# The small block of decays and betas in a hybrid decoder layer: three matmuls a k-tile become two

## The chip, the cores and the metric

The kernel runs on one core of a Trainium2 chip. The metric is the time of one execution on the device in microseconds (us). Before the change three runs gave 2778.44, 2771.64 and 2778.57 us, with a median of 2778.44 us.

The core's engines work side by side, each through its own queue in order: TensorE (PE in the profile; its loading of weights is PEld) multiplies matrices into PSUM, VectorE (DVE) and ScalarE (ACT) work element by element, GpSimd (POOL) does a few small things, and SyncE (SP) issues all the DMA transfers.

## What is computed

One layer with parallel mixers over 2048 tokens and a model width of 1024. A combined projection of the normed input feeds four heads of gated DeltaNet and four of HGRN2; their outputs are concatenated and projected, and an MLP and a gated per-layer embedding follow. The part that matters here are the eight columns of the projection that give each of the four DeltaNet heads its decay and its beta:

```
hn = rms_norm(h, pre_mix_norm)
proj = einsum('btd,dc->btc', hn, w_in)
a_gdn = proj[..., OFF_GDN_A:OFF_GDN_B]      # 4 columns, one a head
b_gdn = proj[..., OFF_GDN_B:OFF_HG_F]       # 4 columns, one a head
beta  = sigmoid(b_gdn)
g_dec = -exp(gdn_a_log) * softplus(a_gdn + gdn_dt_bias)
o_a   = gated_delta_rule_chunked(q_a, k_a, v_a, g_dec, beta)   # uses cumsum(g_dec) inside each chunk
```

All is in float32. A matmul that takes its operands in the rounded form float32r is cheaper but less exact, so the kernel splits every operand into a high part (the value rounded to float32r) and a low part (what the rounding left), both float32r, and sums products of parts.

## The kernel before

**Tiles.** Tokens are cut into four quarters of 512 (`QT`), the 1024 input features into eight k-tiles of 128 (`KD`). The normed input of a quarter stands in eight tiles `xt`, each with a high and a low part side by side. A block of the projection is 128 output columns for one quarter: a bank of PSUM (`mm`) of 128 x 512 receives, for each k-tile, three matmuls: high weights by high input, high weights by low input, low weights by high input. That makes 24 matmuls.

**The list of blocks.** `works` holds, for each quarter, first the block "ab" (decays and betas) and then 32 blocks, eight for each pair of a DeltaNet and an HGRN2 head. [...]

**Weights.** In the first quarter a block's weights are loaded raw, split on ScalarE (a rounding copy, line 163) and VectorE (a subtraction, line 164), and the split tile is stored to DRAM for later (`keep`, line 179). In the other three quarters the split tile is loaded back (`reload`, line 184). There are three buffers for split tiles, so a reload waits until the block three earlier has been multiplied and stored.

**The order of the work.** The orders of TensorE and of SP are written by hand; those of VectorE, ScalarE and GpSimd come from a planner that estimates when each instruction is ready. TensorE's order is woven by a clock: each block is cut into three pieces, and after each piece `tick()` runs the steps that an agenda holds for that beat (and `half()` those for the middle of a piece). The steps of the heads' mixers are generators with fixed beats (`A_STEPS`, `B_STEPS`). So the mixers' small matmuls stand at fixed places among the projection's matmuls, and where a step's input is late, TensorE waits with everything behind it. When the block ab of a new quarter is multiplied, the last DeltaNet head of the quarter before is still in its triangular solve (`pr`, `xs`, lines 662 to 672, on VectorE). Its result goes out to DRAM (`xd`, line 677) and comes back rearranged (`xt`, line 684), VectorE transposes it (`xn`, line 686), and TensorE uses it (`psp`, line 691). The heads that have just finished are normed (`finish`: `og`, `osq`, and `norm_steps`: `hl`, `nrm`, lines 263 and 264).

**From the block to the decays.** `decays` (from line 463) runs in the last beat of the block and in three later ones. ScalarE reads rows 0 to 3 of the bank and adds the bias (`sp`, line 468), VectorE clears the tile `gb` of 36 x 512 (line 469), ScalarE reads rows 32 to 35 and writes their tanh into `gb` (line 470). A softplus follows: `se` = max(-sp, sp) on VectorE (472), an exponential and a logarithm on ScalarE (473, 474; each may need a load of its function's table, ACT_TABLE_LOAD), max and add on VectorE (475), a factor (476), and four running sums along the tokens into `gb` (478). Rows 0 to 3 of `gb` go to DRAM (`gd`, line 482); a copy with part of the tokens turned round (`gbb`, 485) and four small transposes on TensorE (`ps_gb`, 488), due four beats after the block, bring all 36 rows to columns (`gcol`).

The first quarter's block runs right after the start-up in which embeddings are computed: its DMA queue still carries stores of these (`ed`), and VectorE clears the mixers' tiles (lines 417 to 426) once they have landed.

Of the kernel before, what the change touches and what calls it, by code (L numbers as in the profile page):

```python
# [10 lines left out]
F32 = mybir.dt.float32  # L11
# [73 lines left out]
def trunk(ctx, tc, x, xT, pT, vecs, w_in, w_ab, gdn_a_log, gdn_dt_bias, w_out, w_up, w_down,  # L85
# [319 lines left out]
    with mixers as mctx:  # L405
# [6 lines left out]
        def mt(name, tag, bufs=1, shape=(P, NC, P)):  # L412
            return mp.tile(list(shape), F32, tag=tag, name=name, bufs=bufs)
# [49 lines left out]
        def decays(ps, q):  # L463

            gb = mt(f"gb_{q}", "gb", 1, (36, QT))
            sp = m2.tile([4, QT], F32, tag="tmp", name=f"sp_{q}")
            se = m2.tile([4, QT], F32, tag="th", name=f"se_{q}")
            S.activation(sp, ps[0:4, :], AF.Identity, bias=dec[:, 1:2])
            V.memset(gb, 0.0)
            S.activation(gb[32:36, :], ps[32:36, :], AF.Tanh, scale=0.5)  # L470
            V.tensor_scalar(gb[32:36, :], gb[32:36, :], 0.5, 0.5, ALU.mult, ALU.add)
            V.scalar_tensor_tensor(se, sp, -1.0, sp, ALU.mult, ALU.max)
            S.activation(se, se, AF.Exp, scale=-1.0)
            S.activation(se, se, AF.Ln, bias=1.0)
            V.scalar_tensor_tensor(sp, sp, 0.0, se, ALU.max, ALU.add)
            V.tensor_scalar(sp, sp, nexpa, None, ALU.mult)
            for c in range(NC):
                V.tensor_tensor_scan(gb[0:4, blk(c)], one[0:4, :], sp[:, blk(c)], 0.0, ALU.mult, ALU.add)
            gd = dr.tile([4, QT], F32, name=f"gd{q}")
            decay[q] = [gd, None]  # L480
            yield
            nc.sync.dma_start(gd, gb[0:4, :])
            yield
            back = mt(f"gbb_{q}", "gbb", 1, (36, QT // 2))
            V.tensor_copy(back.rearrange("p (n b i) -> p n b i", b=NB, i=SB), odd_back(gb))
            ps = bank(f"ps_gb_{q}", ph)
            for c in range(NC):
                PE.transpose(ps[:, c * 36 : (c + 1) * 36], back[:, blk(c // 2)] if c % 2 else gb[:, blk(c)],
                             ident[:36, :36])
# [435 lines left out]
        last = t + LAST  # L925
        staged, split_w = {}, {}

        def stage_work(j):

            if j < len(works) and works[j][3] == 0:  # L930
                staged[j] = stage(works[j][0], works[j][2])

        def split_work(j):

            if j < len(works):
                split_w[j] = staged.pop(j)() if j in staged else reload(works[j][1], works[j][0])

        def keep_work(j):
            if works[j][3] == 0:
                keep(works[j][1], split_w[j])  # L940

        def load_x(q):
# [68 lines left out]
        with tc.manual_schedule(engines={mybir.EngineType.SP}):  # L1011
            stage_work(0)
            stage_work(1)
            split_work(0)
            stage_work(2)
            split_work(1)
            for j, (name, key, src, q, h, then, g, b) in enumerate(works):
                split_work(j + 2)
                stage_work(j + 3)
                keep_work(j)  # L1020
                ps = bank(f"mm_{name}")
                w, xt = split_w.pop(j), xts[q]
                terms = []
                for k, xk in enumerate(xt):
                    terms += [(w[:, 0, k, :], xk[:, 0, :]), (w[:, 0, k, :], xk[:, 1, :]), (w[:, 1, k, :], xk[:, 0, :])]
                nt = len(terms)
                for s in range(SPT):
                    for i in range(s * nt // SPT, (s + 1) * nt // SPT):
                        if i == (2 * s + 1) * nt // (2 * SPT):
                            half()  # L1030
                        PE.matmul(ps, *terms[i], start=i == 0, stop=i == nt - 1)  # L1031
# [12 lines left out]
            at(clock[0], mix_operands(0), (1, 2, 3, 4, 6, 7, 9, 11))  # L1044
            call(clock[0] + 2, partial(stage_out, 0))
            call(clock[0] + 5, partial(ready_out, 0))
            call(clock[0] + 6, partial(stage_out, 1))
            call(clock[0] + 13, partial(ready_out, 1))
            call(clock[0] + 14, partial(stage_out, 2))
            held = {}  # L1050

            def first_outs():

                for j in range(2):
                    ps = held[j] = bank(f"mmo_0_{j}")
                    w = ready.pop(j)
                    for i in range(3 * KD):
                        k, term = i // 3, i % 3
                        PE.matmul(ps, w[:, term // 2, k, :], xin[0][k][:, term % 2, :], start=i == 0, stop=i == 3 * KD - 1)
                        if i % 8 == 7:  # L1060
                            yield

            outs = first_outs()
            while clock[0] <= last or len(held) < 2 or 1 in ready:
                if fill:
                    q, d = fill.pop(0)
                    new = embed_tile(q, d, ple[d // 4], pts[q], accs, m2, 2)
# [12 lines left out]
                tick()  # L1080
            for _ in outs:
                tick()
# [661 lines left out]
```

## Time and profile before

| | |
|---|---|
| median of three runs | 2778.44 us (2771.64 to 2778.57) |
| span of the profiled execution | 2778.2 us (a time of that execution apart from its span is not given) |
| TensorE busy | 2696.7 us, 97% |
| VectorE busy | 2048.2 us, 74% |
| ScalarE busy | 1471.2 us, 53% |
| matmuls on the block ab | 96 in four blocks, from 44.8, 303.9, 574.6 and 832.4 us |
| bytes moved by DMA | 589.24 MB |

Times in the profile are counted in us from the span's start. A row of the timeline gives start, length, engine, line, operation, output and inputs by the program's names, and in brackets the idle time just before the instruction with what ended it. In the chain of waits a row is one link of the chain that ended last. A matmul's own length in a row is its latency; matmuls follow each other faster than that, since they are pipelined. Windows give each engine's busy time in a stretch, and the clock that TensorE was granted as a share of full speed.

### The profile page before, as it was taken

The page shows a single profiled execution, that of the slowest core. Times are in us where ns is not written, and L with a number is a line of the kernel's source. Part 1 is how long each engine was busy: PE and PEld are TensorE (multiplying, and loading weights), DVE is VectorE, ACT ScalarE, POOL GpSimd, SP SyncE. Part 2 cuts the span into 40 slices and gives each one's busy share as a digit, 9 for nine tenths or more (in the row PEclk, how much of TensorE's full clock was granted, in tenths as well). Part 3 has the DMA queues.
Part 4 walks back from the last instruction along what each step waited for, and adds up shares of the span by engine and source line. Part 5 has one row for each costly group of instructions (what it writes and reads, how often), then busy time and mean ns, then how long its engine had stood idle before and what let it go on. Part 6 is the DMA issues. An engine that isn't in the chain of part 4 may idle for free.

```text
span 2778.2 us, 38362 instructions
## 1 busy us (share of the span) xinstructions
PE 2696.7 (97%) x12721; PEld 2219.1 (80%) x12721; DVE 2048.2 (74%) x4242; ACT 1471.2 (53%) x2943; POOL 104.2 (4%) x104
## 2 busy tenths in 40 slices
PE   7999999999999999999899999999999999999999
PEld 5787788878888887777688887887888888887887
DVE  6787877787787777578889867758787765567775
ACT  6665554455545445676555545545454455465431
POOL 0000000000000000000000000001000000001000
PEclk9999999999999999999999999999999999999999
DMA  7776776667666665887466547667454446577663
GB/s 261 261 242 217 230 249 220 218 215 244 231 211 215 213 213 166 267 300 241 141 222 217 181 149 252 222 192 247 155 197 145 147 165 210 190 254 246 213 207 118
DMA packets 268598, 589.24 MB, mean 212 GB/s; under 512 B 55642, under 2 KB 59960, under 8 KB 249200
## 3 DMA queue, kind: packets, MB, share of 16 engines
q1 hardware_dynamic: 268400, 586.79, 63.2%
q8 instruction: 101, 1.65, 0.2%
q14 instruction: 97, 0.79, 0.1%
HBM read 419.75 MB, written 166.92 MB: 211 GB/s over the span
## 4 chain that ended last, share of the span: by engine, by line
PE 62%; DVE 9%; DMA 8%; issue 6%; ACT 3%; SPq 1%; POOL 1%; DVEq 0%; POOLq 0%; ACTq 0%
PE u L1100 22%; PE d L1100 20%; PE mm L1031 9%; PE mmg L1100 6%; DMA ud_g<-u_g 2%; DMA sys_g<-ud_g 1%; DVE pr_g L667 1%; DVE xs_g L670 1%; DVE xs_g L672 1%; PE mmo L1100 1%; DMA mixT<-mixd 1%; DMA rsb_g<-rd_g 1%; DMA b<-h1d 0%; DMA rd_g<-m_g 0%; DVE acc_vg L511 0%
## 5 line engine op out<-in xcount | busy, mean ns | idle before, releaser
L1031 PE MATMUL mm<-xt,w 128*128 128x512 f32 x3072 | 787.0, 403 | 1.9 <-ACT qk_h L767 0.9
L1031 PEld LDWEIGHTS mm<-xt,w 128*128 128x128 f32 x3072 | 558.6, 190 | 109.7 <-ACT qk_h L767 1.3
L1100 PE MATMUL d<-db,da 128*128 128x512 f32 x2688 | 613.0, 390 | 3.9 <-DVE db L217 1.9
L1100 PE MATMUL u<-t,wu 128*128 128x512 f32 x2604 | 608.0, 396 | 3.3 <-ACT wu L163 3.3
L1100 PEld LDWEIGHTS d<-db,da 128*128 128x128 f32 x2688 | 503.9, 188 | 112.3 <-DVE db L217 4.7
L1100 PEld LDWEIGHTS u<-t,wu 128*128 128x128 f32 x2604 | 489.5, 188 | 121.2 <-ACT wu L163 4.1
L217 DVE TENSOR_TENSOR db<-db 128x512 fp32r<-128x512 f32 x224 | 161.2, 720 | 72.6 <-ACT db L216 71.7
L1429 DVE TENSOR_TENSOR u<-u,u 128x512 f32<-128x512 f32 x224 | 150.3, 682 | 72.5 <-PE u L1100 71.3
L216 ACT ACTIVATE db<-db 128x512 fp32r<-128x512 f32 x224 | 140.9, 629 | 82.2 <-DMA db<-hid 80.2
L1100 PE MATMUL mmo<-mixT,w_out 128*128 128x512 f32 x720 | 172.9, 401 | 7.2 <-DVE w_out L164 5.8
L1100 PE MATMUL mmg<-h2T,wg 128*128 128x512 f32 x768 | 178.1, 394 | 0.0
L1470 ACT ACTIVATE u<-u 128x512 f32<-128x512 f32 x128 | 81.0, 633 | 179.5 <-DVE u L1429 179.0
L1100 PEld LDWEIGHTS mmg<-h2T,wg 128*128 128x128 f32 x768 | 144.3, 188 | 33.5
L1100 PEld LDWEIGHTS mmo<-mixT,w_out 128*128 128x128 f32 x720 | 137.3, 191 | 41.8 <-DVE w_out L164 7.1
L164 DVE TENSOR_TENSOR da<-da 128x512 fp32r<-128x512 f32 x128 | 92.7, 724 | 90.2 <-ACT da L163 89.8
L163 ACT ACTIVATE da<-da 128x512 fp32r<-128x512 f32 x128 | 80.5, 629 | 137.6 <-DMA da<-sumd 113.0
L163 ACT ACTIVATE wu<-a 128x512 fp32r<-128x512 f32 x124 | 74.1, 624 | 47.9 <-DMA a<-in_w_up_dram 45.1
L667 DVE TENSOR_TENSOR pr_g<-xs_g,sys_g 128x16 f32<-128x16 f32 (+14 forms) x240 | 93.8, 391 | 5.4
L227 POOL TENSOR_TENSOR acc_y<-acc_y,sq_y 128x512 f32<-128x512 f32 x28 | 38.4, 1371 | 1393.3 <-ACT sq_y L226 1393.3
L164 DVE TENSOR_TENSOR wu<-a,wu 128x512 fp32r<-128x512 f32 x124 | 84.7, 686 | 4.9 <-ACT wu L163 4.8
L1471 ACT ACTIVATE u<-u 128x512 f32<-128x512 f32 x128 | 80.8, 631 | 3.7
L672 DVE SCALAR_TENSOR_TENSOR xs_g<-xs_g,sys_g 128x4 f32<-128x4 f32 x256 | 57.6, 225 | 29.3 <-DMA sys_g<-ud_g 23.9
(374 smaller groups left out, 3817.6 us busy)
## 6 DMA issues: line engine op xcount, KB each, us to landing
w<-cache_in SPq DMA_DIRECT2D x96, 1024.0 KB
db<-hid SPq DMA_DIRECT2D x224, 256.0 KB
cache_in<-w SPq DMA_DIRECT2D x32, 1024.0 KB
hid<-u SPq DMA_DIRECT2D x128, 256.0 KB
da<-sumd SPq DMA_DIRECT2D x128, 256.0 KB
a<-in_w_up_dram SPq DMA_DIRECT2D x124, 256.0 KB
hid<-ht SPq DMA_DIRECT2D x96, 256.0 KB
dr<-in_w_down_dram SPq DMA_DIRECT2D x96, 256.0 KB
```

The lines of the kernel that those rows point to most:

```text
L163: S.activation(t[:, 0], raw, AF.Copy)
L164: eng.tensor_tensor(t[:, 1], raw, t[:, 0], ALU.subtract)
L216: S.activation(t[:, 0], plain(t), AF.Copy)
L217: V.tensor_tensor(t[:, 1], plain(t), t[:, 0], ALU.subtract)
L227: eng.tensor_tensor(acc, acc, sq, ALU.add)
L667: V.tensor_tensor(pr[:, :, :, 0:i], xs[:, None, :, 0:i].broadcast_to([P, 2, GC, i]), sys[:, 0:i, i : i + 2].rearrange("p j two -> p two j" ...
L672: V.scalar_tensor_tensor(xs[:, :, i + 1], xs[:, :, i], sys[:, i, i + 1 : i + 2], xs[:, :, i + 1], ALU.mult, ALU.add)
L1031: PE.matmul(ps, *terms[i], start=i == 0, stop=i == nt - 1)
L1100: PE.matmul(ps, a, b, start=start, stop=stop)
L1429: V.tensor_tensor(c[new], c[old], ps, ALU.add)
L1470: S.activation(c[k], c[k], AF.Relu)
L1471: S.activation(c[k], c[k], AF.Square)
```

## The change

The eight real columns leave most of the weight tile empty, and the change uses it: the low parts of columns 0 to 35 are put at columns 64 to 99 of the same tile. One matmul with this tile multiplies an input by high and low weights at once, and the results stand in rows 0 to 35 and 64 to 99 of the bank. So a k-tile takes two matmuls (by high and by low input) where it took three, a block 16 where it took 24; the product of low weights and low input, left out before, is now in it. The tile has half the bytes: its store and its three reloads move 0.5 MB each where they moved 1 MB. In the first quarter VectorE subtracts 36 columns a k-tile where it subtracted 128.

`decays` has to add the two groups of rows first: ScalarE copies rows 64 to 99 into `gb`, VectorE adds rows 0 to 35 of the bank, and `sp` and the tanh then read `gb`. The clearing of `gb` goes, since the empty columns give zeros.

```diff
         def decays(ps, q):
             gb = mt(f"gb_{q}", "gb", 1, (36, QT))
+            S.activation(gb, ps[64:100, :], AF.Copy)
+            V.tensor_tensor(gb, gb, ps[0:36, :], ALU.add)
             sp = m2.tile([4, QT], F32, tag="tmp", name=f"sp_{q}")
             se = m2.tile([4, QT], F32, tag="th", name=f"se_{q}")
-            S.activation(sp, ps[0:4, :], AF.Identity, bias=dec[:, 1:2])
-            V.memset(gb, 0.0)
-            S.activation(gb[32:36, :], ps[32:36, :], AF.Tanh, scale=0.5)
+            S.activation(sp, gb[0:4, :], AF.Identity, bias=dec[:, 1:2])
+            S.activation(gb[32:36, :], gb[32:36, :], AF.Tanh, scale=0.5)
...
+        def stage_ab():
+            raw = wp.tile([P, KD, P], F32, tag="raw", name="raw_ab", bufs=2)
+            nc.sync.dma_start(raw, w_ab)
+            def ready():
+                w = wp.tile([P, KD, P], F32R, tag="whl", name="w_ab0")
+                S.activation(w, raw, AF.Copy)
+                V.tensor_tensor(w[:, :, 64:100], raw[:, :, 0:36], w[:, :, 0:36], ALU.subtract)
+                return w
+            return ready
+        def reload_ab(q):
+            w = wp.tile([P, KD, P], F32R, tag="whl", name=f"w_ab{q}")
+            nc.sync.dma_start(w.bitcast(F32).rearrange("p k n -> p (k n)"), cached["ab"])
+            return w
+        def keep_ab(w):
+            cached["ab"] = dr.tile([P, KD * P], F32, name="cache_ab")
+            nc.sync.dma_start(cached["ab"], w.bitcast(F32).rearrange("p k n -> p (k n)"))
...
                 for k, xk in enumerate(xt):
-                    terms += [(w[:, 0, k, :], xk[:, 0, :]), (w[:, 0, k, :], xk[:, 1, :]), (w[:, 1, k, :], xk[:, 0, :])]
+                    if h is None:
+                        terms += [(w[:, k, :], xk[:, 0, :]), (w[:, k, :], xk[:, 1, :])]
+                    else:
+                        terms += [(w[:, 0, k, :], xk[:, 0, :]), (w[:, 0, k, :], xk[:, 1, :]),
+                                  (w[:, 1, k, :], xk[:, 0, :])]
```

`stage_work`, `split_work` and `keep_work` call these functions where the block is ab, at the places where they called `stage`, `reload` and `keep`.

More of the change, by code (lines that the diff above doesn't have):

```diff
@@ L926, in trunk @@
         staged, split_w = {}, {}
+        def stage_ab():
[14 more added lines that the diff above has]
+            nc.sync.dma_start(cached["ab"], w.bitcast(F32).rearrange("p k n -> p (k n)"))
         def stage_work(j):
             if j < len(works) and works[j][3] == 0:
-                staged[j] = stage(works[j][0], works[j][2])
+                staged[j] = stage(works[j][0], works[j][2]) if works[j][4] is not None else stage_ab()
         def split_work(j):
             if j < len(works):
-                split_w[j] = staged.pop(j)() if j in staged else reload(works[j][1], works[j][0])
+                if j in staged:
+                    split_w[j] = staged.pop(j)()
+                else:
+                    split_w[j] = reload(works[j][1], works[j][0]) if works[j][4] is not None else reload_ab(works[j][3])
         def keep_work(j):
-            if works[j][3] == 0:
+            if works[j][3] == 0 and works[j][4] is None:
+                keep_ab(split_w[j])
+            elif works[j][3] == 0:
                 keep(works[j][1], split_w[j])
@@ L1024, in trunk @@
                 for k, xk in enumerate(xt):
-                    terms += [(w[:, 0, k, :], xk[:, 0, :]), (w[:, 0, k, :], xk[:, 1, :]), (w[:, 1, k, :], xk[:, 0, :])]
+                    if h is None:
+                        terms += [(w[:, k, :], xk[:, 0, :]), (w[:, k, :], xk[:, 1, :])]
+                    else:
+                        terms += [(w[:, 0, k, :], xk[:, 0, :]), (w[:, 0, k, :], xk[:, 1, :]),
+                                  (w[:, 1, k, :], xk[:, 0, :])]
                 nt = len(terms)
```

## The prediction

> **What bounds the kernel now.** I read the page first, then the one tile the change is about, then the order of time on each engine around its four appearances. On the page, TensorE is busy for nearly the whole span, so a matmul removed looks like time gained:
>
> ```profile
> span 2778.2 us, 38362 instructions
> PE 2696.7 (97%) x12721; PEld 2219.1 (80%) x12721; DVE 2048.2 (74%) x4242; ACT 1471.2 (53%) x2943; POOL 104.2 (4%) x104
> ```
>
> But that share is a mean over the kernel. The change touches four short places, one a quarter of the tokens, and there the question is what ends TensorE's next wait. The tile's own view gives the size of the block, the chain of waits the pace of its matmuls:
>
> ```profile
> L1031 PE MATMUL mm_ab<-xt,w_ab x96: 388/392/502, 44.8 to 839.1; 128*128 128x512 f32 x96
> L164 DVE TENSOR_TENSOR w_ab<-raw_ab,w_ab x1: 1224/1224/1224, 25.1 to 25.1; 128x1024 fp32r<-128x1024 f32 x1
> 376.70 5.51 PE mm L1031 x24
> ```
>
> The 392 ns is a matmul's latency; 24 in a row take 5.51 us, so one costs 0.230 us of TensorE. Now the last block (fourth quarter), TensorE first (its last row is the same wait in the third quarter), then VectorE, then ScalarE, each in order of time (start, length, engine, line; the idle time before an instruction and who ended it in brackets):
>
> ```profile
> 837.46 2.08 PE L1031 MATMUL mm_ab<-xt,w_ab 128*128 128x512 f32 x8
> 843.54 0.50 PE L264 MATMUL nrm_g<-hl_g,ones 128*128 128x512 f32 x1
> 849.59 0.71 PE L691 MATMUL psp_g<-xn_g,um 128*128 128x128 f32 x4 [0.54 <-DVE xn_g L686]
> ...
> 591.91 0.71 PE L691 MATMUL psp_g<-xn_g,um 128*128 128x128 f32 x4 [0.56 <-DVE xn_g L686]
> ```
> ```profile
> 811.94 0.23 DVE L672 SCALAR_TENSOR_TENSOR xs_g<-xs_g,sys_g 128x4 f32<-128x4 f32 x1 [0.41 <-DMA sys_g<-ud_g]
> 840.17 0.69 DVE L554 TENSOR_TENSOR og_g<-pso_g,zt_zg 128x512 f32<-128x512 f32 x1
> 840.90 0.70 DVE L556 TENSOR_TENSOR osq_g<-osq_g,q_g 128x512 f32<-128x512 f32 x1
> 841.64 0.67 DVE L472 SCALAR_TENSOR_TENSOR se<-sp 4x512 f32<-4x512 f32 x1
> 842.79 0.69 DVE L164 TENSOR_TENSOR hl_g<-osq_g,hl_g 128x512 fp32r<-128x512 f32 x1
> 846.18 0.68 DVE L475 SCALAR_TENSOR_TENSOR sp<-sp,se 4x512 f32<-4x512 f32 x1 [2.54 <-ACT se L474]
> 849.13 0.41 DVE L686 STREAM_TRANSPOSE xn_g<-xt_g 128x256 f32<-128x256 f32 x1
> ```
> ```profile
> 839.58 0.68 ACT L468 ACTIVATE sp<-mm_ab,dec 4x512 f32<-4x512 f32 x1 [0.37 <-PE mm_ab L1031]
> 840.28 0.59 ACT L470 ACTIVATE gb<-mm_ab 4x512 f32<-4x512 f32 x1
> 841.63 0.63 ACT L163 ACTIVATE hl_g<-osq_g 128x512 fp32r<-128x512 f32 x1 [0.75 <-DVE osq_g L556]
> 845.51 0.63 ACT L474 ACTIVATE se<-se 4x512 f32<-4x512 f32 x1
> ```
>
> This is the heart of the case. The block ends at about 839.4. TensorE's next wait (849.59) is for xn_g, which VectorE makes at 849.13, late because VectorE stood still for 2.54 us until ScalarE had the logarithm (845.51 to 846.14): the block's own chain sp, se, table load, exp, table load, ln, sp, scans, all in order on two engines. And sp's partner se started only at 841.64, although sp was there at 840.26: between 811.94 and 846.18 VectorE's rows show no idle time at all. So VectorE's queue, started by a DMA at 811.94, sets when the chain runs; TensorE arrives early and waits. The third quarter repeats this (its wait for xn_g, at 591.91, is 0.56).
>
> **The change part by part.** *Matmuls.* Four blocks of 24 become 16: 32 x 0.230 = 7.4 us of TensorE, 1.84 us a block. If TensorE bounded everywhere, the sum would be -7.4.
>
> *Copy and add ahead of the chain.* The chain gets two instructions. ScalarE's copy of 36x512 out of PSUM is like the gb row above (0.59). VectorE's add with one operand in PSUM is like og_g (0.69): the bounds are 0.49 (the memset of the same 36x512, below) and 0.70 (osq_g), and I take 0.69, the row nearest in operands. Then sp, no longer from PSUM, as before. What is queued behind: the add waits for ScalarE's copy, that for the block's last matmul; behind the add stand og_g, osq_g or se, behind these hl_g, which the norm matmul (843.54) needs. The block's PSUM bank is let go after the add, no later than before. The memset that they replace ran early, off this stretch:
>
> ```profile
> L469 DVE MEMSET gb<- x4: 485/485/485, 53.0 to 597.0; 36x512 f32 x4
> ```
>
> *Blocks three and four (quarters 2, 3 from 0).* The block ends 1.84 us earlier, the copy falls into ScalarE's idle time, but VectorE is full until se: the add pushes osq_g, hl_g, se and through them both table loads by 0.69. TensorE gains 1.84, waits 1.84 + 0.69 more at hl_g and xn_g: +0.7 each. Bounds: had the planner placed add and se ahead of og_g and osq_g (1.3 us of VectorE), the logarithm comes about 1.3 earlier: -1.3; were VectorE no limit at all, -1.84. If the add lands behind osq_g, sp on ScalarE comes behind hl_g and pays its 0.68 as well: +1.4.
>
> *Block two.* Here two things end VectorE's standing almost together:
>
> ```profile
> 318.46 0.17 DVE L664 COPY xs_g<-cst 128x8 f32<-128x8 f32 x1 [3.22 <-DMA xd_g<-xs_g]
> 317.94 0.63 ACT L474 ACTIVATE se<-se 4x512 f32<-4x512 f32 x1
> 322.71 0.71 PE L691 MATMUL psp_g<-xn_g,um 128*128 128x128 f32 x4 [2.35 <-DVE xn_g L686]
> 304.33 8.67 DMA cache_in<-w
> 313.81 0.32 SPq L677 DMA_DIRECT2D xd_g<-xs_g  x1
> ```
>
> The store xd_g lands at 318.46 because SP's queue stood behind a weight reload whose buffer a store (8.67 us from 304.33) still held. Part by part: the reload of the block's weights before it moves 0.5 MB instead of 1 MB, so this goes earlier and stops mattering; the logarithm's end (317.94 + 0.63 = 318.57) moves to 319.26 with the add, where VectorE was free at some 318.7, after the xs_g copy: +0.5. Bounds -1.84 and +1.2 (the add behind osq_g again).
>
> *Block one.* TensorE waits openly for this chain (TensorE, ScalarE, two rows of VectorE, SP, and a window whose last figure is GB/s):
>
> ```profile
> 62.72 0.32 PE L488 MATMUL ps_gb<-cst,gbb 36*128 36x36 f32 x1 [2.83 <-DVE gbb L485]
> 50.65 0.68 ACT L468 ACTIVATE sp<-mm_ab,dec 4x512 f32<-4x512 f32 x1 [3.48 <-PE mm_ab L1031]
> 50.05 0.09 DVE L417 MEMSET bound<- 128x36 f32 x1 [1.43 <-DMA ed<-e]
> 53.36 0.62 DVE L472 SCALAR_TENSOR_TENSOR se<-sp 4x512 f32<-4x512 f32 x1
> 42.36 0.43 SPq L179 DMA_DIRECT2D cache_ab<-w_ab  x1
> 40.00:46.00 6.00, 5.61 (x23) 3.93 (x22) 4.01 (x7) 5.19 (x10) 0.00 (x0) 1.00 0.87 311
> ```
>
> se waits for memsets (50.05 to 53.3, gb's 0.49 among them), and these for the last ed store, queued behind the 1 MB store of this block's weights at 42.36. Half of that at 311 GB/s is 1.7 us, so the memsets can start when VectorE falls idle, 50.05 - 1.43 = 48.6, and last 2.8 without gb's, to 51.4. Then add to 52.1, sp to 52.8, se at 52.85 against 53.36: -0.5. Bounds: -1.84 (add ahead of the memsets), +0.9 (the store lands as before: 52.85, 53.55, 54.25).
>
> *Costing nothing.* The low half of the first weights becomes 288 columns for 1024, saving under 1 us of the 1.22 at 25.1, but VectorE idles next until the norm's row arrives. If VectorE were not idle there, the saving could count in full. The stores and reloads of half the size keep their places in SP's queue, and TensorE's rows on mm_ab show no wait for a reload; where the queue is the limit, blocks one and two have it above.
>
> **Sum**, against this execution's span of 2778.2 (the median of the runs, 2778.44, is 0.2 above it; no separate time of the profiled execution is given): -0.5 + 0.5 + 0.7 + 0.7 = +1.4, so 2779.6 and, on the runs' median, 2779.8: I say 2780. The 7.4 us of matmuls turn into longer waits at hl_g, xn_g and gbb.
>
> **The rivals.** *One: the clock falls in blocks three and four (the slow side of my forecast).* In the windows the second column is TensorE's busy time, and the row ends with granted clock, DMA share and GB/s:
>
> ```profile
> 59.00:63.00 4.00, 0.53 (x4) 0.41 (x4) 3.67 (x10) 3.06 (x5) 2.33 (x1) 0.73 0.30 42
> 63.00:66.00 3.00, 3.00 (x10) 2.35 (x10) 0.82 (x3) 0.34 (x2) 0.27 (x1) 0.50 1.00 375
> 323.00:326.00 3.00, 3.00 (x16) 2.44 (x16) 3.00 (x8) 2.16 (x7) 0.00 (x0) 0.61 1.01 401
> 326.00:329.00 3.00, 3.00 (x13) 2.42 (x12) 1.88 (x7) 1.43 (x3) 0.00 (x0) 0.82 0.98 287
> 849.00:853.00 4.00, 3.41 (x20) 2.75 (x20) 4.00 (x11) 2.44 (x9) 0.00 (x0) 1.00 0.55 35
> ```
>
> After the waits of block one and two TensorE ran at 0.50 and at 0.61 to 0.82; after the short one of block four at 1.00. Block two's fall cost 3 x 0.39 + 3 x 0.18 = 1.7 us. With 2.5 us more waiting, blocks three and four may fall too: 2779.8 + 3.4 = 2783. Against it: the new wait is split by norm matmuls and 16 projections. [...] Chance 0.18.
>
> *Two: the chain does not hold TensorE (the fast side).* The planner lays out VectorE anew and puts add and se ahead of the group's closing work in every block; what decides is whether se starts up to 1.84 us before 841.64, and likewise in the other blocks. Then each block gives up to 1.84: 2778.4 - 7.4 = 2771. For it: copy and block end come early. Against: VectorE's 32 us without a gap up to the logarithm, and sp now needs two hops more. Chance 0.20.
>
> *Three: the order of ScalarE and VectorE is dealt anew beyond the blocks.* Only TensorE's and SP's orders are written by hand. Two quarters with the same work differ, and of the first one's waits one stands out (total us, times, longest):
>
> ```profile
> 304.00:575.00 271.00, 259.99 (x1400) 220.49 (x1399) 203.22 (x589) 138.18 (x364) 15.38 (x17) 0.98 0.69 230
> 575.00:832.00 257.00, 254.12 (x1393) 216.68 (x1392) 198.91 (x582) 137.46 (x363) 15.04 (x17) 1.00 0.67 226
> ```
> ```profile
> PE psc_g L743 <- ACT w_g L740: 6.9, 4, 4.1
> ```
>
> TensorE idles 11.0 us in the second quarter and 2.9 in the third, and most of the 11.0 is the state recurrence: a matmul (psc_g) waits for ScalarE to scale w_g, behind whatever the planner put ahead of it there. If the third quarter came to look like the second, 8 us come on top: 2788; if the fourth did too, 2796. It decides from about 8 us of such waits more, two of the longest (4.1). Chance 0.12; the same luck the other way, the second quarter like the third, 2780 - 8 = 2772 and with some gain of the blocks 2768, 0.05.
>
> **How the numbers follow.** Forecast 0.45, rivals 0.18, 0.20, 0.12 and 0.05. The forecast alone spans 2777 (blocks a little better) to 2784 (near all upper bounds, 0.9 + 1.2 + 1.4 + 1.4 = +4.9). The range for 8 in 10 runs from 2770.5, the full gain, to 2787.5, the clock's fall on top of the upper bounds. A measurement tells about 0.3%, 8.3 us, from nothing: under 2770.1 lie the lucky layout and part of rival two, 0.12; over 2786.8 the unlucky one and the tails of rival one, 0.20; the rest, 0.68, is no measurable change.
>
> **What would show it.** In the changed profile: 64 matmuls on mm_ab; the block's last matmul some 1.8 us nearer its start; an add on VectorE before sp; the psp_g wait near 849.6 and 591.9 grown (or one at nrm_g) to 2 to 3 us together; the wait for gbb in block one at 4 us or more; granted clock after each block. I am wrong if the waits at psp_g and nrm_g stay at half a microsecond (then the gain stands), if se starts before og_g, or if the third and fourth quarter's lengths move by more than 3 us.

## The result, and the profile after

The changed kernel takes 2784.15 us (median of 16 runs, 2778.66 to 2791.21) and the kernel before, beside it, 2778.79 us (16 runs, 2771.64 to 2787.11): a ratio of 1.002 with an interval of 1.001 to 1.0029, or 2.8 to 8.1 us more. The time lies in the predicted range and within the 0.3% called no measurable change, but 5.4 us above the kernel before where the sum said 1.4. It is rival one's 2783 rather than the forecast's 2780.

The profiled execution of the changed kernel took 2780.20 us, with a span of 2778.3, so 1.9 us lie around the span. Profiled executions of one kernel differ by almost as much as the change is worth: a second one of the kernel before had a span of 2774.1, 4.1 less, and one of the changed kernel 2776.2. So the profiles say where time moved, and the medians how much is left of it. The page and the tile's own view, as before:

```profile
span 2778.3 us, 38301 instructions
PE 2690.7 (97%) x12689; PEld 2215.5 (80%) x12689; DVE 2050.2 (74%) x4242; ACT 1473.2 (53%) x2947; POOL 104.0 (4%) x104
```
```profile
L1063 PE MATMUL mm_ab<-xt,w_ab x64: 388/394/499, 45.1 to 834.6; 128*128 128x512 f32 x64
```

The 32 matmuls are gone, and TensorE's busy time is 6.0 us less. The span is the same. The timeline of TensorE, in the last block (from 829.40) and in the third quarter's (from 567.46), shows what stands there instead:

```profile
839.21 0.50 PE L264 MATMUL nrm_g<-hl_g,ones 128*128 128x512 f32 x1 [0.35 <-DVE hl_g L164]
846.83 0.71 PE L692 MATMUL psp_g<-xn_g,um 128*128 128x128 f32 x4 [2.13 <-DVE xn_g L687]
850.32 0.32 PE L489 MATMUL ps_gb<-cst,gbb 36*128 36x36 f32 x1 [2.15 <-DVE gbb L486]
850.79 6.40 PE L1063 MATMUL mm<-xt,w 128*128 128x512 f32 x16
...
585.13 0.71 PE L692 MATMUL psp_g<-xn_g,um 128*128 128x128 f32 x4 [2.10 <-DVE xn_g L687]
588.62 0.32 PE L489 MATMUL ps_gb<-cst,gbb 36*128 36x36 f32 x1 [2.15 <-DVE gbb L486]
589.08 5.87 PE L1063 MATMUL mm<-xt,w 128*128 128x512 f32 x16
```

The predicted wait is the psp_g row: 0.5 before, 2.1 now. The next wait, at ps_gb, did not exist in these two blocks. And the 16 projections behind it take 6.40 and 5.87 us, where the kernel before took 3.95 in the last block: the clock fell. The kernel before, in the last block:

```profile
851.07 0.23 PE L488 MATMUL ps_gb<-cst,gbb 36*128 36x36 f32 x1
851.35 3.95 PE L1031 MATMUL mm<-xt,w 128*128 128x512 f32 x16
```

The windows around the fall in the changed kernel's last block (TensorE's busy time in the second column; granted clock, DMA share and GB/s at the end):

```profile
846.00:849.00 3.00, 1.34 (x9) 1.10 (x9) 3.00 (x10) 0.86 (x4) 0.00 (x0) 1.00 0.11 38
849.00:852.00 3.00, 1.68 (x6) 1.42 (x7) 2.08 (x8) 2.25 (x4) 0.00 (x0) 0.55 0.59 45
852.00:856.00 4.00, 4.00 (x11) 3.11 (x10) 0.69 (x2) 0.07 (x1) 0.00 (x0) 0.50 0.93 365
```

VectorE and then ScalarE in the last block of the changed kernel show how the chain came to be late:

```profile
836.83 0.67 DVE L557 TENSOR_TENSOR osq_g<-osq_g,q_g 128x512 f32<-128x512 f32 x1
837.75 0.66 DVE L467 TENSOR_TENSOR gb<-gb,mm_ab 36x512 f32<-36x512 f32 x1
839.41 0.67 DVE L473 SCALAR_TENSOR_TENSOR se<-sp 4x512 f32<-4x512 f32 x1
844.67 0.68 DVE L476 SCALAR_TENSOR_TENSOR sp<-sp,se 4x512 f32<-4x512 f32 x1 [1.52 <-ACT se L475]
846.35 0.42 DVE L687 STREAM_TRANSPOSE xn_g<-xt_g 128x256 f32<-128x256 f32 x1
846.71 1.32 DVE L479 TENSOR_TENSOR_SCAN gb<-one,sp 4x128 f32<-4x128 f32 x4
847.96 0.71 DVE L512 SCALAR_TENSOR_TENSOR acc_kg<-mm,cols,acc_kg 128x510 f32<-128x510 f32 x1
...
849.99 0.27 DVE L486 COPY gbb<-gb 36x256 f32<-36x256 f32 x1
```
```profile
837.53 0.63 ACT L163 ACTIVATE hl_g<-osq_g 128x512 fp32r<-128x512 f32 x1 [1.36 <-DVE osq_g L557]
838.45 0.72 ACT L470 ACTIVATE sp<-gb,dec 4x512 f32<-4x512 f32 x1 [0.28 <-DVE gb L467]
839.85 0.59 ACT L266 ACTIVATE osq_g<-nrm_g 1x512 f32<-1x512 f32 x1
840.45 1.28 ACT L474 ACT_TABLE_LOAD   x1
842.28 0.41 ACT L828 ACTIVATE keys_h<-qk_h 128x256 f32<-128x256 f32 x1
844.01 0.63 ACT L475 ACTIVATE se<-se 4x512 f32<-4x512 f32 x1
```

The add stands behind osq_g, and sp behind hl_g. Operations that were not in the chain's way before now are. On ScalarE the pass osq_g (line 266) runs ahead of the exponential's table load (before, it ran at 846.17, behind the logarithm), and keys_h between the exponential and the logarithm's table load. On VectorE two pieces of the convolution (acc_kg) and more stand between the scans and gbb, from 847.96 to 849.99. Counted from each block's first matmul, the last block reads:

| us after the block's first matmul | before | after | difference |
|---|---|---|---|
| last matmul of the block starts | 6.73 | 5.16 | -1.57 |
| logarithm ends | 13.72 | 15.24 | +1.52 |
| psp_g starts | 17.16 | 17.43 | +0.27 |
| scans end | 16.77 | 18.63 | +1.86 |
| gbb starts | 17.87 | 20.59 | +2.72 |
| last ps_gb starts | 18.77 | 21.16 | +2.39 |
| first key product (kk_g) starts | 35.49 | 40.38 | +4.89 |

The block gets 1.6 us shorter, not 1.84 (1.8 in block one, 1.2 in block two). The logarithm is 1.5 later, yet psp_g only 0.3: the planner put the transposition xn_g ahead of the scans (846.35, 846.71), and gbb paid for it. From ps_gb to kk_g another 2.5 us are lost to the clock.

### The profile page after: what moved, and what is told of

It is laid out like the page before. It is cut to its first block, busy times and chain, and to the rows that moved or that the text cites. A ratio compares the mean times of both kernels' runs of the same rounds, so it can differ in the third digit from the quotient of the medians.

```text
span 2778.3 us, 38301 instructions
## 1 busy us (share of the span) xinstructions
PE 2690.7 (97%) x12689; PEld 2215.5 (80%) x12689; DVE 2050.2 (74%) x4242; ACT 1473.2 (53%) x2947; POOL 104.0 (4%) x104
## 4 chain that ended last, share of the span: by engine, by line
PE 63%; DVE 11%; DMA 7%; ACT 4%; issue 4%; SPq 1%; POOL 1%; DVEq 0%; ACTq 0%; POOLq 0%
PE u L1132 22%; PE d L1132 18%; PE mm L1063 11%; PE mmg L1132 6%; DMA ud_g<-u_g 1%; DVE pr_g L668 1%; DMA sys_g<-ud_g 1%; PE mmo L1132 1%; DVE xs_g L671 1%; DVE xs_g L673 1%; DMA rd_g<-m_g 1%; DMA da<-sumd 1%; DVE raw_xt L980 1%; DMA xs<-in_x_dram 1%; DVE xt L164 1%
## 5 line engine op out<-in xcount | busy, mean ns | idle before, releaser
L1132 PEld LDWEIGHTS mmg<-h2T,wg 128*128 128x128 f32 x768 | 144.2, 188 | 33.8 <-issue 0.4
L164 DVE TENSOR_TENSOR da<-dr,da 128x512 fp32r<-128x512 f32 x96 | 66.3, 690 | 18.3 <-ACT da L163 16.3
```

The source lines that it names most:

```text
L164: eng.tensor_tensor(t[:, 1], raw, t[:, 0], ALU.subtract)
L1132: PE.matmul(ps, a, b, start=start, stop=stop)
```

## The experiments

The measure used below is the time from a block's first matmul on mm_ab to the first head's key product kk_g behind it, in the four blocks in turn. A second profile of the kernel before told how far it varies on its own.

| | blocks one to four, us | from block one's kk_g to block two | ratio to before |
|---|---|---|---|
| before | 33.9, 38.3, 35.6, 35.5 | 225.3 | |
| before, second profile | 34.6, 38.1, 35.6, 35.3 | 222.4 | |
| after | 33.4, 39.8, 40.1, 40.4 | 220.1 | 1.0020 |
| after, second profile | 34.1, 40.1, 40.6, 39.7 | 220.3 | |

> The kernel before once more, for a second profile of it. In its first profile the stretches between the blocks (first quarter, second quarter) took 225.3 and 232.4 us, in the changed kernel and the three experiments 217.6 to 220.1 and 226.7 to 229.1. If that difference belongs to the kernel, it is there again; if it was that execution's own (falls of the clock at other places, DMA), this one has about 219 and 228. The times from a block's start to the first head's key products should be the same again: 38.3, 35.6 and 35.5 us in blocks two to four.

The blocks repeat within 0.7 us; the rest of the first quarter does so only within 3. The two stretches between blocks took 222.4 and 230.1 us, between what the two readings said, so how much of their difference belongs to the kernel is left open. The second profile of the changed kernel asked whether its falls of the clock were chance:

> The changed kernel once more, unaltered, for a second profile. Theory A (the granted clock falls in blocks three and four because TensorE has little to do for some 4 us there: the gap ahead of the preparation's transposes, the transposes, the gap ahead of the weights' transposes): the falls behind 586 and 849 us come again within 10 us of those places, and the times from the block's first matmul to the first head's key products are again about 39.8, 40.1 and 40.4 us for blocks two to four (each within 0.7). Theory B (the falls of that one execution were chance): no fall behind one or both of the places, and that block takes about 37 us, as blocks three and four took 38.2 and 36.5 in the kernel with the early copy of the weights' rows.

They came again, at 585.9 and 845.3 us and 6.8 us long each, and the block times with them (block two's fall was 6.8 us for 3.4). Theory A held. The falls are not the profiled executions' own either: over all 16 runs of the changed kernel the mean granted clock is 0.9902, and over the kernel before 0.9928 to 0.9932 beside the experiments.

**The two halves of the change, each alone.** The chain (run e1): copy and add in the kernel before, with its 24 matmuls.

```diff
+            S.activation(gb, ps[64:100, :], AF.Copy)
+            V.tensor_tensor(gb, gb, ps[0:36, :], ALU.add)
-            S.activation(sp, ps[0:4, :], AF.Identity, bias=dec[:, 1:2])
-            V.memset(gb, 0.0)
-            S.activation(gb[32:36, :], ps[32:36, :], AF.Tanh, scale=0.5)
+            S.activation(sp, gb[0:4, :], AF.Identity, bias=dec[:, 1:2])
+            S.activation(gb[32:36, :], gb[32:36, :], AF.Tanh, scale=0.5)
```

> Only the copy and the add are put ahead of the chain; weights, 24 matmuls a block and transfers stay as before (the rows 64 to 99 that are added are zeros here). Theory A (the longer chain makes TensorE wait, and the waits let its clock fall): in blocks two to four the transposes on gb come about 21 us after the block's start, as in the changed kernel, for 18.8 before, whatever the number of matmuls; so 3 x 2.4 us more, block one some 1 us more, and 0 to 2 falls of the clock of 3.4 us each: 2787 to 2795 beside 2779 for the kernel before. Theory B (the two instructions cost what they last, 1.3 us each block, and the matmuls' saving stands in full elsewhere): 2784. Theory C (the two instructions are hidden in a block of 24 matmuls): 2779.

2792.19 against 2777.41 us, a ratio of 1.0056 (1.0038 to 1.0074): +14.8 us, for instructions that last 0.60 + 0.67 us and come four times. Theory A's 2787 to 2795 holds. The blocks took 36.7, 42.1, 41.6 and 41.4. TensorE in the last block, and the window behind:

```profile
849.79 0.71 PE L692 MATMUL psp_g<-xn_g,um 128*128 128x128 f32 x4 [0.81 <-DVE xn_g L687]
855.49 0.32 PE L489 MATMUL ps_gb<-cst,gbb 36*128 36x36 f32 x1 [3.65 <-DVE gbb L486]
```
```profile
856.00:860.00 4.00, 4.00 (x12) 3.17 (x12) 1.85 (x5) 1.22 (x4) 0.00 (x0) 0.57 1.02 426
```

So the loss is the chain's. In this block it sits at gbb (ps_gb is done 4.2 us later than before) and in the clock (1.7 more from there to kk_g), not at psp_g. The matmuls (run e2): two a k-tile, the old chain and the tile of 1 MB.

```diff
-                    terms += [(w[:, 0, k, :], xk[:, 0, :]), (w[:, 0, k, :], xk[:, 1, :]), (w[:, 1, k, :], xk[:, 0, :])]
+                    terms += [(w[:, 0, k, :], xk[:, 0, :]), (w[:, 0, k, :], xk[:, 1, :])]
+                    if h is not None:
+                        terms += [(w[:, 1, k, :], xk[:, 0, :])]
```

> Only the matmuls: 16 a block (the product with the low weights is left out for decays and betas), the chain and the transfers as before. Theory A: in blocks two to four VectorE and the chain still end where they ended, TensorE comes 1.84 us early and waits for it at xn_g and gbb; little is gained, and the wait at psp_g (2.35, 0.56, 0.54 before) grows to 2 to 4 us; with one or two more falls of the clock 2777 to 2784. Theory B: the saving stands, 2771.5 to 2773, and the waits at psp_g stay at half a microsecond in blocks three and four.

2773.51 us, 0.9985 (0.9973 to 0.9996): 3.9 us less. That misses theory A's 2777 to 2784 and is next to theory B's 2773, but the blocks are as theory A had them: 34.2, 39.5, 35.0, 35.0, in sum 143.8 where the kernel before had 143.2 and 143.5. In blocks three and four 0.2 to 0.6 of the 1.84 arrived, in the first two nothing. The gain lies behind blocks one and two (220.0 us for 225.3 and 222.4, 228.1 for 232.4 and 230.1), and no term explains it. One row of TensorE says why the blocks gained so little:

```profile
842.43 0.71 PE L691 MATMUL psp_g<-xn_g,um 128*128 128x128 f32 x4 [1.49 <-DVE xn_g L686]
```

psp_g starts 17.03 us after the block's first matmul, before 17.16: the block's last matmul comes 1.5 us earlier (5.19 for 6.73), and the waits take 1.4 of it back, 0.95 at psp_g (0.54 to 1.49) and 0.46 at nrm_g. That is the prediction's main mechanism, measured alone. The two halves sum to +10.9 where the change gives +5.4, so the parts do not simply add; that they share the same waits is argued, not shown by a run of its own.

**The new wait and the fall behind it.** Run e3: eight matmuls without use ahead of ps_gb's transposes, 1.84 us of TensorE inside the wait for gbb:

```diff
             ps = bank(f"ps_gb_{q}", ph)
+            for i in range(8):
+                PE.matmul(ps, ones, xts[q][i][:, 0, :], start=True, stop=True)
```

> The changed kernel with eight matmuls of 128x512 whose results nobody reads, put right ahead of the transposes on gb (1.84 us of TensorE a block, inside the wait for gbb of 2.2 to 2.7 us). Theory A, the clock's share: the falls after blocks three and four (6.8 us at half speed each, 3.4 us lost) shrink or go, so 2777 to 2781, below the changed kernel's 2784 although it has more to multiply. If the clock is not what costs, the time stays at 2784, or rises by up to 4 x 1.84 where TensorE was not waiting: 2784 to 2791.

2780.68 us, 1.0012 (1.0002 to 1.0023). More work, and blocks two to four are shorter: 33.6, 38.3, 39.1, 38.0. The last block had no fall, nor had block two:

```profile
846.00:850.00 4.00, 3.71 (x18) 2.71 (x17) 2.98 (x10) 2.53 (x5) 0.00 (x0) 1.00 0.62 44
850.00:854.00 4.00, 4.00 (x26) 3.51 (x25) 0.96 (x2) 1.33 (x5) 0.00 (x0) 1.00 1.03 422
```

By this profile 2.4 us of the last block's +4.9 belong to the clock: from ps_gb to kk_g it takes 16.7 us, as before the change. Over the 12 runs of e3 the mean granted clock is 0.9928 again, that of the kernel before. But the interval of the ratio overlaps that of the changed kernel, so the clock's share of the whole time is not measured by it. Next the wait itself (run e5): the copy gbb written right behind the scans.

```diff
+            back = mt(f"gbb_{q}", "gbb", 1, (36, QT // 2))
+            V.tensor_copy(back.rearrange("p (n b i) -> p n b i", b=NB, i=SB), odd_back(gb))
             yield
             nc.sync.dma_start(gd, gb[0:4, :])
             yield
-            back = mt(f"gbb_{q}", "gbb", 1, (36, QT // 2))
-            V.tensor_copy(back.rearrange("p (n b i) -> p n b i", b=NB, i=SB), odd_back(gb))
```

> The changed kernel with the copy gbb written in the program right behind the running sums, in the step that makes them, for three beats later. Theory A, the order's share: the planner then puts it ahead of the convolution's three operations and the masks (2 us of VectorE between the sums' end and gbb in blocks three and four); the transposes' wait for gbb falls from 2.15 to under 0.5 us in blocks two to four, and fewer falls of the clock follow: 2770 to 2778. If the order on VectorE is not what holds TensorE, the time stays at 2784 and another wait takes its place.

2777.25 us, 0.9997 (0.9987 to 1.0007): one moved copy takes the loss back, as theory A said. Blocks 33.8, 36.3, 38.2, 36.5; the wait at ps_gb in the last block goes from 2.15 to 0.76 (under 0.5 was expected), and of blocks two to four the clock falls in block three only, for 3.4 us. That profile is of the quickest of the 12 runs, 2770.33 us at a mean clock of 0.994; over all 12 the clock is 0.9912, so most runs had more falls than it shows.

```profile
838.95 0.25 PE L489 MATMUL ps_gb<-cst,gbb 36*128 36x36 f32 x1 [0.76 <-DVE gbb L483]
```

**Later instead of earlier.** The steps of decays at later beats, so that TensorE works on before it comes to ps_gb (run e4); e6 does this together with the early copy.

```diff
-                        at(clock[0], decays(ps, q), (0, 2, 4, 5))
+                        at(clock[0], decays(ps, q), (0, 2, 6, 7))
```

> The changed kernel with the transposes on gb two beats (16 matmuls, 3.7 us of TensorE) later. Theory A: gbb is there by then, the wait of 2.2 to 2.7 us for it goes in blocks two to four (block one keeps some 1 us of its 5), the falls of the clock after blocks three and four go with it: ratio to the kernel before 0.997 to 0.9995, 2770 to 2776. If the wait only moves to the next step that needs gcol or to the convolution's output, the time stays at the changed kernel's ratio, 1.002.

> The gbb copy early and the transposes two beats later, both. Theory A: as the later transposes alone, no more than 1 us better in blocks two to four, because either alone takes the wait away; block one gains up to 3 us by the later transposes: ratio 0.996 to 0.999. If gbb's place on VectorE matters for more than this wait (it delays the convolution by 0.3 us), no better than the later transposes alone.

The gain did not come: 2781.5 us, 1.0022 (1.0013 to 1.0032), and 2781.23 us, 1.0019 (1.001 to 1.0028). The blocks are short, 27.5, 35.7, 35.7, 35.6 in e4 and 27.5, 35.4, 37.3, 35.7 in e6, but in e4 from block one's key products to block two it takes 235.4 us where the changed kernel takes 220.1. The first quarter, whose weights are loaded raw and split, was 6 us ahead and stood still later (timeline, then a window, of e4):

```profile
104.85 11.23 PE L1063 MATMUL mm<-xt,w 128*128 128x512 f32 x38 [2.49 <-DVE w L164]
126.58 1.23 PE L692 MATMUL psp_g<-xn_g,um 128*128 128x128 f32 x4 [5.49 <-DVE xn_g L687]
```
```profile
106.00:110.00 4.00, 4.00 (x12) 3.08 (x11) 3.63 (x11) 1.06 (x1) 0.00 (x0) 0.53 0.96 329
```

The clock fell three times there, 6.8 us each. So the same edit was made for the blocks behind the first alone (run e8), and once more in the kernel before as a control (run e10):

```diff
-                        at(clock[0], decays(ps, q), (0, 2, 4, 5))
+                        at(clock[0], decays(ps, q), (0, 2, 6, 7) if q else (0, 2, 4, 5))
```

> The changed kernel with the decays' four steps at offsets 0, 2, 6, 7 in the blocks behind the first, and 0, 2, 4, 5 in the first as it is. Theory A (in blocks two to four the chain of decays and betas is what TensorE waits for, and with the later offsets those waits and the falls of the clock go; the 9.5 us that the kernel with all four blocks later lost lay in its first quarter alone): from the block's first matmul to the first head's key products about 35.7 us in each of blocks two to four, and 33.4 in the first; against the changed kernel 4 us less in each of three blocks, some of it given back behind them, so 2771 to 2776 us, a ratio to the kernel before of 0.996 to 0.999. Theory B (a block that is ahead gives it back in its own quarter, wherever the block lies, as the first quarter did): the blocks are as short as under A, but the quarters behind them are longer by as much, and the ratio is 1.000 to 1.003.

> The kernel before, with the decays' steps at offsets 0, 2, 6, 7 in the blocks behind the first. It tells whether what the later offsets gained in the changed kernel is the changed kernel's own loss taken back, or a gain that any kernel of this kind has. Theory A (the former): the kernel before waits only 0.5 us ahead of these blocks' weights' transposes and its clock does not fall in blocks three and four, so there is nothing to take back: 35.0 to 35.8 us from the block's first matmul to the first head's key products in blocks three and four as before, up to 2.5 us less in block two, and a ratio to the kernel before of 0.999 to 1.001. Theory B (the latter): a microsecond or more less in each of the three blocks, a ratio of 0.996 to 0.9985.

The changed kernel: 2774.02 against 2777.34 us, 0.9993 (0.9983 to 1.0002), blocks 33.8, 35.4, 35.7, 35.4, and no fall in blocks two to four. The median is where theory A had it; the ratio is just above its range (the two medians alone give 0.9988). The profile is again of the quickest run, 2769.88 us; over all 12 the mean clock is 0.9925. The kernel before: 2777.88 against 2775.69 us, 1.0007 (0.9998 to 1.0016), blocks 34.2, 38.1, 35.6, 35.6; nothing to take back, as theory A said, though block two gained 0.2 us (0 against the second profile) of the 2.5 that it allowed. TensorE in the last block of the changed kernel with later beats, a window of it, and the same wait of the control:

```profile
842.03 0.71 PE L692 MATMUL psp_g<-xn_g,um 128*128 128x128 f32 x4 [2.11 <-DVE xn_g L687]
```
```profile
844.00:848.00 4.00, 4.00 (x25) 3.50 (x23) 2.46 (x9) 3.03 (x7) 0.00 (x0) 1.00 0.74 128
```
```profile
844.30 0.71 PE L691 MATMUL psp_g<-xn_g,um 128*128 128x128 f32 x4 [0.53 <-DVE xn_g L686]
```

The psp_g wait of 2.1 us is still there, and the block is no longer than before the change. What cost the time were the wait at ps_gb and the clock, not psp_g.

**A shorter chain.** In run e7 the copy adds the bias itself, sp has no pass of its own, and gbb is early as above:

```diff
-            S.activation(gb, ps[64:100, :], AF.Copy)
+            S.activation(gb, ps[64:100, :], AF.Identity, bias=gbias)
...
-            S.activation(sp, gb[0:4, :], AF.Identity, bias=dec[:, 1:2])
...
-            V.scalar_tensor_tensor(se, sp, -1.0, sp, ALU.mult, ALU.max)
+            V.scalar_tensor_tensor(se, gb[0:4, :], -1.0, gb[0:4, :], ALU.mult, ALU.max)
...
-            V.scalar_tensor_tensor(sp, sp, 0.0, se, ALU.max, ALU.add)
+            V.scalar_tensor_tensor(sp, gb[0:4, :], 0.0, se, ALU.max, ALU.add)
```

> The gbb copy early, and the chain one instruction shorter: the copy adds the bias too, so sp's own pass on ScalarE (0.72 us) goes and VectorE takes max and add straight from gb. Theory A (chain length sets the wait at xn_g and gbb): the logarithm comes 0.7 us earlier in blocks two to four, psp_g's wait shrinks from 2.1 to about 1.4, ratio 0.9985 to 0.9995 for 0.9997 with gbb early alone. If VectorE's queue and not the chain is what counts, the same 0.9997.

> Both: the bias added in the copy of the one group of rows, with no pass of its own for it; the copy of the weights' rows written right behind the scans; and the later offsets in the blocks behind the first. Theory A (the two act on the same waits, and the clock stays up in blocks two to four once the waits are short): about 35.3 us from the block's first matmul to the first head's key products in blocks two to four, and 33.7 in the first; 2768 to 2773 us, a ratio of 0.9955 to 0.998. Theory B (the bias' kernel has already what can be had of these waits, and the later offsets only put the chain's end later): the blocks as in the bias' kernel or longer, a ratio of 0.998 to 1.001.

2772.49 us, 0.9984 (0.9975 to 0.9993), for e7: faster than both kernels, though its interval overlaps that of e5. Theory A's way there did not come true. The logarithm ends 0.8 to 1.2 us earlier than in e5, but the wait at psp_g shrinks in block two only (1.56 to 0.71) and grows from 2.1 to 2.6 us in blocks three and four, where the planner now puts the scans ahead of xn_g (VectorE in the last block):

```profile
842.37 1.34 DVE L481 TENSOR_TENSOR_SCAN gb<-one,sp 4x128 f32<-4x128 f32 x4
843.64 0.41 DVE L689 STREAM_TRANSPOSE xn_g<-xt_g 128x256 f32<-128x256 f32 x1
```

The blocks, 33.7, 37.3, 39.3, 37.7, are longer than e5's, with a fall in each of the last three, so where e7's gain lies is not shown. With later beats in addition (e9), 2772.49 us, 0.9984 (0.9973 to 0.9994), blocks 33.4, 34.8, 37.9, 37.9: nothing more, so there theory B is nearer. In e9 the wait for xn_g is 2.57, ps_gb has none, and that one wait is followed by a fall of 3.4 us in blocks three and four (timeline, window):

```profile
841.54 0.96 PE L694 MATMUL psp_g<-xn_g,um 128*128 128x128 f32 x4 [2.57 <-DVE xn_g L689]
```
```profile
842.00:845.00 3.00, 3.00 (x12) 2.61 (x11) 2.47 (x7) 2.39 (x6) 0.00 (x0) 0.50 0.78 51
```

## Why the prediction was right, and where it was not

**The heart: right.** VectorE's queue and the chain on it, not the block's length, set when xn_g is there. VectorE's stretch with next to no idle time starts 20.5 us before the last block's first matmul in the kernel before (811.94) and in the changed kernel (808.87), and 20.6 in e2 (804.83). What was saved in a block went into the waits at nrm_g and psp_g, in the changed kernel and, with nothing else altered, in e2; it was 1.5 to 1.6 us in blocks three and four, where the sum had 1.84. Rival two needed the chain not to hold TensorE; se does start before 841.64, by 2.2 us, but it stands behind og_g and osq_g, and the logarithm ends only 1.5 us earlier in absolute time, in a block that began 3.0 earlier.

**Blocks three and four: +0.7 each predicted, +4.5 and +4.9 measured.** Two terms failed. The add was taken to push the chain by 0.69, and se does come 0.9 and 0.8 us later after the block's start; but the logarithm is 1.6 and 1.5 later. The order that the text had as its upper bound came true (add behind osq_g, sp behind hl_g, +1.4). Its price is near by luck: sp waited for the add, not for hl_g, and the rest came from ScalarE, where sp, the tanh and osq_g now stand between hl_g and the exponential's table load and keys_h ahead of the logarithm's. And the sum followed the chain to xn_g and stopped there. "Where a stall goes, what is late next" was gbb, a copy behind the scans that TensorE uses 1.5 us after psp_g. It came 2.7 later: the scans end 1.9 later, behind xn_g, and the planner put 0.9 us more of VectorE between them and gbb. That wait, 2.15 us, was in no term. e5 and e8, which shorten it to 0.76 and remove it, bring the ratio back to 0.9997 and 0.9993.

**The clock: the rival, not the forecast.** Rival one foresaw the fall in blocks three and four at 1.7 us a block, from 2.5 us more waiting. The waits grew by some 4 us a block, the clock fell in both profiles of the changed kernel, and a fall cost 1.8 to 2.5 us there (from ps_gb to kk_g). That the time came out next to rival one's 2783 is in part luck: the blocks alone are 10.5 us longer, where rival one had 4.8 in all, and about half came back elsewhere. No single wait was long there: 2.10 and 2.15 us in block three, 2.13 and 2.15 in block four, each pair with 1.3 us of small work between, were enough. In blocks one and two before the change, where the clock fell too, the longest were 2.83 and 2.35. The length of one wait does not decide it: behind 2.11 us at psp_g the clock fell in block three of e6, and behind 2.12 in block three of e8 it did not. The last section shows what told them apart.

**Block two: +0.5 predicted, +1.5 measured (+2.0 in the second profiles).** VectorE's copy of xs_g no longer waits for the store xd_g, as was said of the smaller reload. That wait varies, though: it was 3.22 us in the first profile of the kernel before and 1.03 in the second, and with the tile of 1 MB it was 0.16 in e1 and 1.49 in e2. The first of the next two rows is VectorE's:

```profile
310.41 0.17 DVE L665 COPY xs_g<-cst 128x8 f32<-128x8 f32 x1
```
```profile
319.99 0.25 PE L489 MATMUL ps_gb<-cst,gbb 36*128 36x36 f32 x1 [2.74 <-DVE gbb L486]
```

psp_g comes 1.4 earlier after the block's start (17.35 for 18.79), better than the sum had it, and gbb 1.9 later.

**Block one: -0.5 predicted, -0.4 measured, by another way.** The wait is what was said, 4.0 + 0.95 us, "4 us or more". But the memsets began at 49.39, not 48.6, and a split of weights came between add and se:

```profile
52.15 0.62 DVE L467 TENSOR_TENSOR gb<-gb,mm_ab 36x512 f32<-36x512 f32 x1
52.70 1.20 DVE L164 TENSOR_TENSOR w<-raw,w 128x1024 fp32r<-128x1024 f32 x1
53.83 0.67 DVE L473 SCALAR_TENSOR_TENSOR se<-sp 4x512 f32<-4x512 f32 x1
```

se starts at 53.83 for 53.36, late by 0.5 instead of early by 0.5 (0.15 late after the block's start, which itself came 0.3 later). That the number fits is luck. What paid for it is that gbb here follows the scans at once (17.07 to 17.11 us after the start; before, 15.75 to 17.61).

**Given back.** The four blocks together are 10.5 us longer in the first pair of profiles and 11.0 in the second; the medians differ by 5.4. The rest came back mostly behind blocks one and two: 220.1 and 220.3 us for 222.4 to 225.3, and 229.1 and 224.7 for 230.1 and 232.4. In the first quarter a late block one costs little: from block one's start to block two's it takes 253.5 us after, 254.3 in e1 (with 24 matmuls, 1 MB and the longest block one) and 257.0 and 259.1 before. In e2, with the old chain, it takes 254.2. So neither the matmuls, the bytes nor the chain alone explains it. Behind block one TensorE idled 11.4 us in the first profile of the kernel before and 7.5 in the second, which has a fall of the clock at 220.0 us in this stretch; the changed kernel idled 7.4 and 7.6 without one. What makes the difference stays open.

**Quarters and order.** One of the signs that the prediction named against itself did appear: from block three's start to block four's it takes 261.9 us for 257.8, 4.2 more where 3 was the limit. All of it is in the block (+4.5); behind it stand 221.8 us for 222.2. The orders of VectorE and ScalarE differ from those of the kernel before around the four blocks only, so rival three did not happen.

## What to carry to other kernels

A chain that is lengthened on two busy engines is to be followed past its first consumer: to every later reader of its result, and to what a planner can push in between. In the last block TensorE waited twice within 5.6 us (2.13 and 2.15 us), the waits counted together, and with the clock's fall the loss doubled (2.4 us at ps_gb, 4.9 at kk_g). Moving the second reader's input forward (one copy here) or its beat back took 0.23% and 0.27% off the changed kernel's ratio, where the 32 matmuls alone had brought 0.15%. And getting ahead is no gain in itself: in e4 block one was 6 us shorter, and the rest of the first quarter lost that and 9 us more in later waits and three falls of the clock. That the loads of the weights set the pace there is argued, not shown.

## What the hardware showed beside that

The granted clock fell to 0.5 for 3.4 or for 6.8 us each time in these blocks, except for one 10.2 in e1; no fall had another length.

In each of the 14 profiles all falls begin whole multiples of 3.41 us apart, as if on a grid; in the first profiles of the two kernels the step is 3.413 us, and no fall lies more than 0.02 us off it. Cut into windows of that grid (from 40 us on, without the last 8 us), the traces show what a fall follows. Behind each of the 84 windows at full clock in which TensorE was busy for less than 1.5 us, the clock fell; behind windows with 1.5 to 2.25 us it fell 19 times in 143, and behind the 10810 busier ones never (in the first profiles of the two kernels 14 times in 14, once in 20 and never in 1540). So the same wait cost a fall or not by how it lay to the grid. The two waits of 2.11 and 2.12 us at psp_g, in block three of e6 and then of e8, each with the window behind it:

```profile
589.85:593.27 3.42, 1.31 (x9) 0.88 (x8) 2.92 (x7) 1.41 (x5) 0.00 (x0) 1.00 0.57 240
593.27:596.68 3.41, 3.41 (x11) 2.76 (x10) 3.00 (x9) 2.23 (x6) 0.00 (x0) 0.50 0.15 26
```
```profile
582.03:585.44 3.41, 2.07 (x13) 1.89 (x14) 3.41 (x9) 0.94 (x5) 0.00 (x0) 1.00 0.22 88
585.44:588.86 3.42, 3.42 (x21) 2.92 (x20) 1.93 (x7) 2.54 (x5) 0.00 (x0) 1.00 0.30 65
```

In the falls of the first profiles one projection follows another in 0.427 us (block one before the change, blocks one, three and four after it), at full clock in 0.230. A fall of 6.8 us would so cost some 3.1 us if TensorE were busy all through it, an estimate from these two numbers where the expectation of e3 has 3.4; where it began inside a wait it cost 1.8 to 2.5 us, in the changed kernel's blocks three and four. The falls differ between executions of one kernel elsewhere (there is one at 220 us in one profile of the kernel before and not in the other), so a single profile's clock is evidence only where it repeats.

That float32r is cheaper can be read beside the projections: a product in plain float32 with 128 columns (at_h, kk_g, psp_g) is two records 0.11 us apart, 0.22 us in all, about what a projection in float32r takes for 512 columns (0.230). How much less exact it is, no run shows.
